# The last two column blocks of a down projection as a seven-product pair, a smaller scratch for GpSimd's DMAs, and what takes its place

## The chip, the cores and the metric

The kernel runs on one core of a Trainium2 chip. The metric is device time in microseconds (us) of one execution; the median of three runs stands for the kernel. The core's engines are TensorE (PE, with its weight loads as PEld), VectorE (DVE), ScalarE (ACT), GpSimd (POOL) and SyncE (SP). Each runs its own instructions in a fixed order and waits on semaphores of the others. In this kernel SP issues the loads of weights, POOL those of a few other things.

## The reference

One layer of a hybrid decoder on 256 tokens of width 2048, all in float32: two gated attention branches, an output projection and a feed-forward block with a causal convolution of width 3.

```python
for l in range(DEPTH):
    h = rms_norm(x, norm_mix_pre[l])
    y = hybrid_mixer(h, w_in[l], ...)            # latent attention + sliding window, gates, w_out
    x = x + rms_norm(y, norm_mix_post[l])
    h = rms_norm(x, norm_ffn_pre[l])
    y = conv_ffn(h, ffn_w_up[l], ..., ffn_w_down[l])
    x = x + rms_norm(y, norm_ffn_post[l])

def conv_ffn(h, w_up, conv_w, conv_b, w_down):
    a, b = jnp.split(h @ w_up, 2, axis=-1)
    ap = jnp.pad(a, ((0, 0), (CONV_WIDTH - 1, 0), (0, 0)))
    c = conv_b
    for j in range(CONV_WIDTH):
        c = c + conv_w[j] * ap[:, j:j + S]
    return (jax.nn.gelu(c, approximate=True) * b) @ w_down
```

The last product, with `w_down` (5632 x 2048), is the down projection. 5632 is 44 rows of 128, 2048 is 4 column blocks of 512.

## The kernel before

**Products.** The 256 tokens are two tiles of 128 (`NT` = 2, index `t`). A float32 operand is split into a high and a low part, and `mm3` adds three matmuls into an accumulator: high by high, high by low, low by high. "A product" below is one `mm3`: 128 rows of weights, one token tile, 512 columns.

**Weights.** They arrive as raw chunks [128 x 1024] of float32, 512 KB each. SP issues the load (L141 or L161), ACT casts the high part (`whi`, L153), DVE subtracts to get the low part (`wlo`, L154), then PE uses both. Raw chunks come from a ring and from lists of further tiles (`more_raw`); converted chunks from a ring of four, with one or two flexible places.

**Pairs of column blocks.** `pair_gemm` (L255) computes two column blocks at once, so that four accumulators (two token tiles by two blocks) are open. Its order string has a letter for each two rows of weights. "p" is a plain unit: two chunks, 8 products, 24 matmuls. "s" is a seven-product unit after Strassen's scheme: 7 products, 21 matmuls. It needs sums of the activations (`g_sums`, `b_sums`, made on DVE) and differences of the weights; it converts three whole chunks and a half. In `seven_parked` the differences were made much earlier and lie in DRAM: `park_sums` (L224) has POOL load two chunks to a staging tile (`load`, L230), four subtractions on DVE (`less`, L234) and POOL store two tiles (L239, L244). At the pair's end four extra accumulators are combined by eight column operations on DVE and ACT (`end_sums`).

**Down projection.** Rows 0 to 23 are done when half of the feed-forward's columns are there, as two pairs ("d0", "d1", with the orders in `PAIR_ORDER`, parked tiles `ta`). Rows 24 to 43 come at the end of the program: blocks 0 and 1 as the pair "db" (`B_ORDER`, six seven-product units, parked tiles `tb`), then block 2 and block 3, each by a plain `gemm` through `down`. After it come, for each token tile, the squares and gains of the second norm (`z_block`), the sum of squares (`z_pre`), the normaliser and the four results with their stores (`finish`). For the second token tile the last block is split, so that its last three rows are done in two halves of 256 columns.

**What sets the order.** `at(tick, f)` puts a piece of work to a tick, and each weight chunk calls `tick()`. Within that the framework's scheduler sets each engine's order from the program's order, priorities and when buffers are free; the result is static. A tile whose buffer is free from the start may so be loaded long before its tick.

**Scratch.** A part of each SBUF partition is set aside for descriptors of DMAs that GpSimd issues; 16 KB by default.

Of the kernel before, what the change touches and what calls it, by code (L numbers as in the profile page):

```python
# [19 lines left out]
P = 128  # L20
# [22 lines left out]
def trunk_layer(ctx, tc, x, x_cols_in, conv_cols_in, g_mix_post, g_ffn_post, w_in, w_q, w_kv,  # L43
# [74 lines left out]
    raw_of = lambda name: ring_tile("raw", name, F32, False)  # L118

# [135 lines left out]
    def pair_gemm(name, w, k0, c0, order, act_of, s_of, kind, d, place=None, sums=None, parked=None):  # L255
# [9 lines left out]

        def plain(u, last):
            for k in (2 * u, 2 * u + 1):
                w_ = convert(raw_row(row(k)), 1024)
                for t in range(NT):
                    for j in range(2):  # L270
                        mul(c[2 * t + j], act_of(k, t), half(w_, j), last and k % 2 == 1)
                tick()

        def seven_parked(u, last):
# [13 lines left out]
            w_ = convert(raw_row(parked[u][1]), 1024)  # L288
            mul(q6, s2, half(w_, 1), last)
            mul(c21, act_of(2 * u + 1, 1), half(w_, 0))  # L290
# [4 lines left out]
        def seven(u, last):  # L295
# [18 lines left out]
            w_ = convert(tb, 1024)  # L314
            mul(q6, s2, half(w_, 0), last)
# [464 lines left out]

    es1.close()
# [29 lines left out]
    tb[1], tb[2] = gate_pair(1)  # L811
    parked_a = [park_a(i, pg, "gr", now[0] + 5 + 5 * i, bufs=2) for i in range(EARLY)]
# [148 lines left out]

    b = now[0] + 2
# [362 lines left out]
    def deep_raws():  # L1325
        turn_flex("w")
        more_raw[:] = [raw_of, f_raw("a"), raw_of, f_raw("b"), raw_of, f_raw("a"), f_raw("b")]

    turn_flex("raw")
    at(now[0] + 8, deep_raws)  # L1330
# [19 lines left out]
    parked_b = [park_sums(f"tb{i}_", w_down, 24 + 2 * i, 0, p6, "gp", now[0] + 6 + 8 * i) for i in range(NB_)]  # L1350
# [11 lines left out]
    def z_block(acc, b, t):  # L1362
# [7 lines left out]
        vec.tensor_tensor(zo, z, gpost2[c0 // 1024][:, c0 % 1024:c0 % 1024 + n], op=ALU.mult)  # L1370
# [12 lines left out]
    def finish(t):  # L1383
# [8 lines left out]
        cuts = range(0, D + 1, 512)  # L1392
        for a, b in zip(cuts[:-1], cuts[1:]):
            vec.scalar_tensor_tensor(dsum_all[t][:, a:b], dsum_all[t][:, a:b], r[:, 0:1], x2_all[t][:, a:b], op0=ALU.mult, op1=ALU.add)
            nc.sync.dma_start(out[t * P:(t + 1) * P, a:b], dsum_all[t][:, a:b])

# [11 lines left out]
    def pair_end(i):  # L1408
        t, j = divmod(i, 2)
        vec.tensor_tensor(dsum[t][j], dsum[t][j], ud[i], op=ALU.add)  # L1410
        z_block(c_db[i], j, t)
# [7 lines left out]
    for i in range(4):  # L1419
        at(now[0] + 2 * i, lambda i=i: pair_end(i))  # L1420
    for i in range(8):
        at(now[0] + 2 * i, lambda i=i: unpark(i // 4, i % 4))
    for j in range(2, 4):
        last = j == 3
        acc, todo = down(24, 20, 512 * j, 512, split=5 if last else None, ps=None if last else (pss, "s"))
        if last:
            z_block(acc[0], 3, 0)
            z_pre(0)
            z_block(acc[0], 4, 0)
            part = [pss.tile([P, 512], F32, name="zb0", tag="s")] + [pst.tile([P, 512], F32, name=f"zb{i}", tag="t") for i in (1, 2)]  # L1430
# [102 lines left out]
```

## Time and profile before

| what | value |
|---|---|
| median of 3 runs | 1461.35 us (1460.38 to 1462.37) |
| the profiled execution | 1461.99 us |
| its span in the profile | 1460.2 us |
| mean granted TensorE clock | 0.999 |
| PE / DVE / ACT / POOL busy | 99 / 77 / 58 / 7% |
| weight chunks of 1024 columns converted on DVE | 501 |
| HBM traffic over the span | 230 GB/s |

The span is the time from the profile's first to its last instruction; the profiled execution's time is longer by what lies around it (1.8 us). In timelines a row has start, duration, engine, source line, operation and tiles, and in brackets the idle time before it and who ended it. A row with "x4" is four instructions run together. Matmuls overlap: the step from one start to the next (the pitch) is what each costs. In the view of windows the columns are length, then busy time of PE, PEld, DVE, ACT and POOL with their instructions, the granted clock, the DMA engines' share and GB/s.

### The profile page before, as it was taken

How to read it: one execution, taken by the hardware profiler on the slowest of the kernel's cores; microseconds unless marked ns; L12 is line 12 of the kernel's file. 1: busy time of each engine (PE TensorE's matmuls, PEld its weight loads, DVE VectorE, ACT ScalarE, POOL GpSimd, SP SyncE). 2: the span in 40 equal slices, each digit the busy share in tenths (PEclk: the TensorE clock that was granted, in tenths of full speed). 3: DMA queues.
4: the chain of work that ended last, by engine and by line, in shares of the span. 5: the costliest groups of instructions: out<-in, count | busy, mean ns of one | idle time of the engine just before them, and what ended most of it. 6: DMA issues, size and time to landing. Idle time of an engine off the chain costs nothing.

```text
span 1460.2 us, 21246 instructions
## 1 busy us (share of the span) xinstructions
PE 1449.6 (99%) x7546; PEld 1238.6 (85%) x7546; DVE 1117.3 (77%) x1953; ACT 850.2 (58%) x1401; POOL 96.4 (7%) x172
## 2 busy tenths in 40 slices
PE   9999999999999999999999999999999999999997
PEld 7888888888888888888888888888888888888886
DVE  7788896766667665768789888876768798876776
ACT  7588874543555554446576565655646565655653
POOL 0012110010000001000000011000000100000000
PEclk9999999999999999999999999999999999999999
DMA  8765376698655559765766789756878888667873
GB/s 303 213 173 164 100 263 195 219 324 257 189 156 160 167 162 333 256 204 163 235 226 213 260 294 315 230 185 221 284 269 299 303 273 296 193 189 252 310 246 130
DMA packets 162438, 336.65 MB, mean 231 GB/s; under 512 B 20075, under 2 KB 31244, under 8 KB 162332
## 3 DMA queue, kind: packets, MB, share of 16 engines
q1 hardware_dynamic: 145600, 276.46, 59.1%
q0 software_dynamic: 16640, 58.78, 11.8%
q8 instruction: 59, 0.97, 0.3%
q14 instruction: 47, 0.39, 0.1%
q10 hardware_dynamic: 92, 0.05, 0.0%
HBM read 308.99 MB, written 26.26 MB: 230 GB/s over the span
## 4 chain that ended last, share of the span: by engine, by line
PE 94%; DVE 3%; ACT 2%; issue 1%; DMA 1%; DVEq 0%; ACTq 0%
PE accg L185 11%; PE accg L187 11%; PE accg L186 11%; PE ub L1263 10%; PE ua L1263 10%; PE ub L1267 5%; PE ua L1267 5%; PE cd L187 2%; PE cd L186 2%; PE cd L185 2%; PE mpo L950 1%; PE cdb L187 1%; PE cdb L185 1%; PE cdb L186 1%; PE cg L185 1%; PE cg L187 1%
## 5 line engine op out<-in xcount | busy, mean ns | idle before, releaser
L154 DVE TENSOR_TENSOR wlo<-raw,whi 128x1024 fp32r<-128x1024 f32 (+2 forms) x485 | 575.3, 1194 | 214.7 <-ACT whi L153 207.3
L153 ACT CAST whi<-raw 128x1024 fp32r<-128x1024 f32 (+2 forms) x485 | 495.0, 1027 | 384.2 <-PE accg L187 155.0
L185 PE MATMUL accg<-whi,ahl 128*128 128x512 f32 (+1 forms) x416 | 162.8, 391 | 0.0
L187 PE MATMUL accg<-whi,ahl 128*128 128x512 f32 (+1 forms) x416 | 160.6, 386 | 0.0
L186 PE MATMUL accg<-wlo,ahl 128*128 128x512 f32 (+1 forms) x416 | 159.8, 384 | 0.0
L1263 PE MATMUL ub<-ahl,whi 128*128 128x512 f32 x640 | 154.7, 391 | 0.1
L1263 PE MATMUL ua<-ahl,whi 128*128 128x512 f32 x640 | 154.6, 391 | 0.0
L185 PE MATMUL accg<-whi,bhl 128*128 128x512 f32 x378 | 148.1, 392 | 0.0
L187 PE MATMUL accg<-whi,bhl 128*128 128x512 f32 x378 | 147.4, 390 | 0.0
L186 PE MATMUL accg<-wlo,bhl 128*128 128x512 f32 x378 | 147.3, 390 | 0.0
L1263 PEld LDWEIGHTS ub<-ahl,whi 128*128 128x128 f32 x640 | 117.5, 188 | 23.0 <-ACT cc L1155 0.4
L1263 PEld LDWEIGHTS ua<-ahl,whi 128*128 128x128 f32 x640 | 117.5, 188 | 22.7
L187 PEld LDWEIGHTS accg<-whi,ahl 128*128 128x128 f32 x416 | 78.1, 188 | 15.4
L186 PEld LDWEIGHTS accg<-wlo,ahl 128*128 128x128 f32 x416 | 78.2, 188 | 13.1
L185 PEld LDWEIGHTS accg<-whi,ahl 128*128 128x128 f32 x416 | 78.2, 188 | 12.9
L1267 PEld LDWEIGHTS ub<-ahl,wlo 128*128 128x128 f32 x640 | 82.3, 191 | 3.2
L1267 PEld LDWEIGHTS ua<-ahl,wlo 128*128 128x128 f32 x640 | 82.2, 191 | 3.1
L1267 PE MATMUL ua<-ahl,wlo 128*128 128x256 f32 x640 | 83.7, 283 | 0.0
L187 PEld LDWEIGHTS accg<-whi,bhl 128*128 128x128 f32 x378 | 71.0, 188 | 14.8
L1267 PE MATMUL ub<-ahl,wlo 128*128 128x256 f32 x640 | 83.3, 283 | 0.0
L186 PEld LDWEIGHTS accg<-wlo,bhl 128*128 128x128 f32 x378 | 71.0, 188 | 14.4
L185 PEld LDWEIGHTS accg<-whi,bhl 128*128 128x128 f32 x378 | 71.0, 188 | 14.4
(575 smaller groups left out, 2417.4 us busy)
## 6 DMA issues: line engine op xcount, KB each, us to landing
raw<-in_ffn_w_up_dram SPq DMA_DIRECT2D x137, 512.0 KB, 4.8
raw<-in_w_in_dram SPq DMA_DIRECT2D x105, 512.0 KB, 4.6
raw<-in_ffn_w_down_dram SPq DMA_DIRECT2D x71, 512.0 KB, 5.0
xraw<-in_ffn_w_up_dram SPq DMA_DIRECT2D x39, 512.0 KB, 5.4
raw<-in_w_o_swa_dram SPq DMA_DIRECT2D x32, 512.0 KB, 5.1
raw<-in_w_o_mla_dram SPq DMA_DIRECT2D x32, 512.0 KB, 5.3
raw<-in_w_out_dram SPq DMA_DIRECT2D x26, 512.0 KB, 4.2
ta_s<-in_ffn_w_down_dram POOLq DMA_DIRECT2D x22, 512.0 KB, 6.1
```

Of the source, the lines that this page charges most:

```text
L153: act.copy(hi[:, a:b], raw[:, a:b])
L154: vec.tensor_tensor(lo[:, a:b], raw[:, a:b], hi[:, a:b].bitcast(F32), op=ALU.subtract)
L185: pe.matmul(o, ah, bh, start=start, stop=False)
L186: pe.matmul(o, ah, bl, start=False, stop=False)
L187: pe.matmul(o, al, bh, start=False, stop=stop)
L950: pe.matmul(o, w(t), p_[:, c], start=n == 0, stop=n == 5)
L1263: pe.matmul(acc[i], hi[:, c], hn[p][:, j * 512:(j + 1) * 512], start=p + j == 0, stop=stop)
L1267: pe.matmul(acc[i][:, 0:256], lo[:, c], hn[p][:, j * 512:j * 512 + 256], start=False, stop=False)
```

## The change

1. *Last two blocks as a pair.* Blocks 2 and 3 of rows 24 to 43 become a third call, "dc", with `B2_ORDER` "ppsspssppp": four seven-product units. Its four parked pairs of differences (`tc`) are made in the attention stage. The activation sums of "db" are used again. The last six chunks are applied to the first token tile only, and kept (`held`); the second tile's products with them are done at the end by `rest`.
2. *One more unit in the first half:* `PAIR_ORDER[0]` goes from "ppppspsspssp" to "pppspsspsssp", with one more parked pair, also in the attention stage. Two of its activation sums are made one column block earlier.
3. *Memory.* The scratch is set to 4096 bytes. In the 12 KB stand a staging tile (`STAGE`, 8 KB in each partition, tag "sg"), used by the later parks in place of a shared one, and a raw chunk (`raw_x`, 4 KB, tag "rx"), added to the lists of raw chunks.
4. *The end.* `z_block` may put its gains later; the column work of "db" is done over four ticks rather than eight, and the residual's reloads (`unpark`) at ticks 8 and 14 of "dc". `finish(0)` leaves two of its four results to be done within the second tile's last `z_block`.

```diff
+    raw_f = lambda name: ring_tile("raw", name, F32, True)
+    raw_x = lambda name: sb(base, [P, 1024], name, tag="rx")
...
-    def convert(raw, n, own=None, parts=None):
+    def convert(raw, n, own=None, parts=None, into=None):
...
-        if own:
+        if into:
+            hi, lo = into
+        elif own:
...
+        chunks, hold = [2 * order.count("p")], len(held) if held else 0
+        left = [order.count("s")]
...
         def plain(u, last):
             for k in (2 * u, 2 * u + 1):
-                w_ = convert(raw_row(row(k)), 1024)
+                chunks[0] -= 1
+                w_ = convert(raw_row(row(k)), 1024, into=into() if hold and chunks[0] == hold - 1 else None)
                 for t in range(NT):
+                    if t and chunks[0] < hold:
+                        held[hold - 1 - chunks[0]] = (act_of(k, 1), w_)
+                        continue
                     for j in range(2):
-                        mul(c[2 * t + j], act_of(k, t), half(w_, j), last and k % 2 == 1)
+                        mul(c[2 * t + j], act_of(k, t), half(w_, j),
+                            chunks[0] == (hold if t else 0) and (j == 1 or not left[0]))
...
+    STAGE = dict(pl=base, tag="sg")
...
+    parked_b2 = []
...
+    for i in range(NB2):
+        parked_b2.append(park_sums(f"tc{i}_", w_down, 24 + 2 * i, 1024, t0=now[0] + 7 + 7 * i, **STAGE))
+    parked_a.append(park_a(EARLY, t0=now[0] + 7 + 7 * NB2, **STAGE))
...
-        more_raw[:] = [raw_of, lambda name: t[:, 0:1024], raw_of, lambda name: t[:, 1024:2048], raw_of]
+        more_raw[:] = [raw_of, lambda name: t[:, 0:1024], raw_of, lambda name: t[:, 1024:2048], raw_of, raw_x]
...
-    for i in range(sum(NA) - EARLY):
-        parked_a.append(park_a(i + EARLY, p6, "gp", now[0] + 8 + 15 * i // 2))
+    for i in range(sum(NA) - EARLY - 1):
+        parked_a.append(park_a(i + EARLY + 1, t0=now[0] + 8 + 15 * i // 2, **STAGE))
...
-            for u in range(2):
-                at(now[0] + 3 + 3 * u, lambda u=u: g_sums(u))
+            for u, t in ((0, 3), (1, 6), (4, 10), (5, 14)):
+                at(now[0] + t, lambda u=u: g_sums(u))
...
-            for u, t in ((4, 0), (5, 4), (2, 8), (3, 11)):
+            for u, t in ((2, 8), (3, 11)):
                 at(now[0] + t, lambda u=u: g_sums(u))
...
     turn_flex("raw")
+    more_raw[:] = [raw_of, raw_x, raw_of, raw_f, raw_of, raw_f]
...
+        def result(j):
+            a, b = 512 * j, 512 * j + 512
+            ins = vec.scalar_tensor_tensor(dsum_all[t][:, a:b], dsum_all[t][:, a:b], r[:, 0:1], x2_all[t][:, a:b], op0=ALU.mult, op1=ALU.add)
+            if j in late:
+                tc.keep_in_program_order(ins)
             nc.sync.dma_start(out[t * P:(t + 1) * P, a:b], dsum_all[t][:, a:b])
...
     for i in range(4):
-        at(now[0] + 2 * i, lambda i=i: pair_end(i))
+        at(now[0] + i, lambda i=i: pair_end(i))
     for i in range(8):
-        at(now[0] + 2 * i, lambda i=i: unpark(i // 4, i % 4))
-    for j in range(2, 4):
...
+        at(now[0] + (8, 14)[i // 4] + i % 4, lambda i=i: unpark(i // 4, i % 4))
+    held = [None] * 6
...
+    c = pair_gemm("dc", w_down, 24, 1024, B2_ORDER, lambda k, t: (GH(k)[:, t * P:(t + 1) * P], GL(k)[:, t * P:(t + 1) * P]),
+                  lambda u: sb_of[u], 1, ud2_tiles, parked=parked_b2, held=held,
+                  into=lambda: [sb(base, [P, 1024], f"wh{k}", F32R, tag=f"ahl{k}") for k in (6, 7)])
+    z_block(c[0], 2, 0)
+    z_block(c[1], 3, 0)
+    z_pre(0)
+    z_block(c[1], 4, 0)
+    for j in range(2):
+        vec.tensor_tensor(dsum[1][2 + j], dsum[1][2 + j], c[2 + j], op=ALU.add)
...
+    rest(part[0], held, 0, 512)
+    z_block(part[0], 2, 1)
+    rest(part[1], held[:-3], 512, 1024)
+    vec.tensor_tensor(dsum[1][3], dsum[1][3], part[1], op=ALU.add)
+    for i in range(2):
+        rest(part[2 + i], held[-3:], 512 + i * 256, 768 + i * 256)
+    rest_of_0 = finish(0, (2, 3))
+    z_block(part[2], 3, 1)
+    z_pre(1)
+    z_block(part[3], 4, 1, rest_of_0)
     finish(1)
...
+B2_ORDER = "ppsspssppp"
+NB2 = B2_ORDER.count("s")
...
-PAIR_ORDER = ("ppppspsspssp", "ppspspsspssp")
+PAIR_ORDER = ("pppspsspsssp", "ppspspsspssp")
...
-    nc = _bacc.Bacc("TRN2", target_bir_lowering=False, num_devices=1)
+    nc = _bacc.Bacc("TRN2", target_bir_lowering=False, num_devices=1, dynamic_dma_scratch_size=4096)
```

The scheduler's order shows what stands where. **At the program's start** SP has the first loads of the input projection; raw_201 is the second row of weights, raw_224 the third, `xr` are columns of the input. Before:

```order
L141 DMA raw_201<-in_w_in_dram 128x2x512
L407 DMA xr_129<-in_x_cols_dram 128x256
L141 DMA raw_224<-in_w_in_dram 128x2x512
L407 DMA xr_130<-in_x_cols_dram 128x256
L141 DMA raw_245<-in_w_in_dram 128x2x512
```

and now:

```order
L143 DMA raw_201<-in_w_in_dram 128x2x512
L421 DMA xr_129<-in_x_cols_dram 128x256
L143 DMA raw_8782<-in_ffn_w_up_dram 128x2x512
L143 DMA raw_224<-in_w_in_dram 128x2x512
L421 DMA xr_130<-in_x_cols_dram 128x256
```

A chunk of the feed-forward's weights (raw_8782, into `raw_x`) has come ahead of raw_224. POOL, in the same place, `gmat` being the norms' gains and `strip` the bias table. Before:

```order
L434 MEMSET ones 128x1
L528 COPY gmat<-gx 128x38
L461 DMA strip<-sel 32x384
L611 DMA bias_646<-strip 128x2x256
L611 DMA bias_734<-strip 128x2x256
```

and now:

```order
L448 MEMSET ones 128x1
L542 COPY gmat<-gx 128x38
L234 DMA tc_s<-in_ffn_w_down_dram 128x1024 x2
L475 DMA strip<-sel 32x384
L625 DMA bias_646<-strip 128x2x256
```

The two loads for the first parked pair of "dc" have become POOL's first DMAs.

**At the program's end** DVE works through the norm. ds_7660 (now ds_7715) holds the first token tile's sums and then results, ds_7661 (now ds_7716) the second's; zb are PE's last accumulators, z the sums that are squared, rz the normaliser. Before:

```order
L1391 SCALAR_TENSOR_TENSOR rz_14281<-wz_14280,yz_14279 128x1
L1394 SCALAR_TENSOR_TENSOR ds_7660<-ds_7660,rz_14281,x2b_13873 128x512 x4
L1433 TENSOR_TENSOR ds_7661<-ds_7661,zb_14234 128x512
L1367 TENSOR_TENSOR z_1_14295<-ds_7661,zb_14235 128x256
L1370 TENSOR_TENSOR ds_7661<-z_1_14295,gpost_1_13368 128x256
L1367 TENSOR_TENSOR z_1_14303<-ds_7661,zb_14236 128x256
L1379 TENSOR_REDUCE zpre_13365<-ssz_13363 128x1
L1370 TENSOR_TENSOR ds_7661<-z_1_14303,gpost_1_13368 128x256
```

and now:

```order
L1418 SCALAR_TENSOR_TENSOR rz_14403<-wz_14402,yz_14401 128x1
L1387 TENSOR_TENSOR z_1_14413<-ds_7716,zb_14348 128x256
L1422 SCALAR_TENSOR_TENSOR ds_7715<-ds_7715,rz_14403,x2b_14121 128x512 x2
L1390 TENSOR_TENSOR ds_7716<-z_1_14413,gpost_1_13437 128x256
L1406 TENSOR_REDUCE zpre_13434<-ssz_13432 128x1
L1387 TENSOR_TENSOR z_1_14421<-ds_7716,zb_14349 128x256
L1407 TENSOR_SCALAR zpre_13434<-zpre_13434 128x1
L1422 SCALAR_TENSOR_TENSOR ds_7715<-ds_7715,rz_14403,x2b_14121 128x512
L1408 TENSOR_SCALAR zpre_13434<-zpre_13434 128x1
L1422 SCALAR_TENSOR_TENSOR ds_7715<-ds_7715,rz_14403,x2b_14121 128x512
L1390 TENSOR_TENSOR ds_7716<-z_1_14421,gpost_1_13437 128x256
```

The first tile's four results stood ahead of the second tile's last sums; now two stand between the last-but-one and the last of these, and two behind the last.

More of the change, by code (lines that the diff above doesn't have):

```diff
@@ L253, in park_a, with pair_gemm @@
         return park_sums(f"ta{i}_", w_down, 2 * u, 1024 * p, pl, tag, t0, **kw)
-    def pair_gemm(name, w, k0, c0, order, act_of, s_of, kind, d, place=None, sums=None, parked=None):
+    def pair_gemm(name, w, k0, c0, order, act_of, s_of, kind, d, place=None, sums=None, parked=None, held=None, into=None):
         c11, c12, c21, c22 = c = banks(kind, f"c{name}_")
@@ L288, in seven_parked @@
             w_ = convert(raw_row(parked[u][1]), 1024)
+            left[0] -= 1
             mul(q6, s2, half(w_, 1), last)
-            mul(c21, act_of(2 * u + 1, 1), half(w_, 0))
+            mul(c21, act_of(2 * u + 1, 1), half(w_, 0), last and 0 < hold == chunks[0])
             tick()
@@ L1348, in b_sums @@
         sb_of[u] = token_sums(gtiles[u].bitcast(F32), a, m, hi, lo)
-    parked_b = [park_sums(f"tb{i}_", w_down, 24 + 2 * i, 0, p6, "gp", now[0] + 6 + 8 * i) for i in range(NB_)]
+    parked_b = [park_sums(f"tb{i}_", w_down, 24 + 2 * i, 0, t0=now[0] + 6 + 8 * i, **STAGE) for i in range(NB_)]
     for c in range(6, 11):
```

60 lines of the change are left out of this document (31 added, 29 removed).

## The prediction

> **What bounds the kernel now.** I read the page first, for which engine fills the span, then what that engine waits for, then single places at the two ends.
>
> ```profile
> span 1460.2 us, 21246 instructions
> ...
> PE 1449.6 (99%) x7546; PEld 1238.6 (85%) x7546; DVE 1117.3 (77%) x1953; ACT 850.2 (58%) x1401; POOL 96.4 (7%) x172
> ...
> PE 94%; DVE 3%; ACT 2%; issue 1%; DMA 1%; DVEq 0%; ACTq 0%
> ```
>
> TensorE is busy 99% of the span and makes 94% of the chain that ended last. The view of waits for PE has three lines in all:
>
> ```profile
> PE warm L78 <- DVE ramp L67: 1.1, 1, 1.1
> PE x2T L1073 <- DVE x L1070: 0.8, 1, 0.8
> PE pstrip L420 <- DMA sel<-in_strip_sel_dram: 0.2, 1, 0.2
> ```
>
> So between the first weights and the last product PE waits 0.8 us in one place, and never for a weight. Two rules follow. A matmul removed anywhere shortens the span by its pitch, provided the weights stay ahead. And a stall added anywhere lengthens it by the whole stall, since PE has no idle time in which to make it up. Outside PE's stretch lie the start (until weights are there) and the tail after PE's last product. The profiled execution took 1461.99 us for a span of 1460.2 us; it lies 0.6 us above the median 1461.35. I put my differences onto the median.
>
> **What is removed.** A seven-product unit makes with 7 products what a plain unit makes with 8, and a product is three matmuls of 512 columns. The order strings hold five more such units (one in pair 0 of the first half, four in the last two blocks): 15 matmuls fewer. The number of 256-column matmuls at the end stays 18. The pitch comes from the chain of waits:
>
> ```profile
> 1340.03 3.65 PE ub L1263 x16
> ```
>
> 3.65/16 = 228 ns, and 15 x 0.228 = **3.4 us** less. It is exact if nothing waits; there is no way to gain more on PE.
>
> **What is added to weight traffic and to DVE.** A seven-product unit converts 3.5 chunks where a plain one converts 2, and each parked pair costs four subtractions. By form (busy us, mean ns):
>
> ```profile
> L154 DVE TENSOR_TENSOR wlo<-raw,whi 128x1024 fp32r<-128x1024 f32 x456 | 555.3, 1223 | 212.1 <-ACT whi L153 205.3 <-PE ua L1263 1.5 <-DMA raw<-in_mla_w_q_up_dram 1.5
> L153 ACT CAST whi<-raw 128x1024 fp32r<-128x1024 f32 x456 | 476.6, 1051 | 375.6 <-PE accg L187 154.3 <-PE cd L187 37.4 <-PE ua L1263 28.3
> ...
> L234 DVE TENSOR_TENSOR ta_s<-ta_s 128x512 f32<-128x512 f32 x44 | 30.2, 685 | 7.0 <-DMA ta_s<-in_ffn_w_down_dram 6.7
> ```
>
> DVE gains 5 x (1.5 x 1.223 + 4 x 0.685) = 22.9 us, ACT 5 x 1.5 x 1.051 = 7.9 us. All of it must lie under PE. The stages it falls into (us; busy of PE, PEld, DVE, ACT, POOL; granted clock, DMA share, GB/s):
>
> ```profile
> 380.00:400.00 20.00, 20.00 (x129) 17.93 (x129) 14.98 (x27) 10.82 (x21) 1.08 (x2) 1.00 0.59 180
> ...
> 1345.00:1397.00 52.00, 52.00 (x233) 43.14 (x233) 41.25 (x51) 33.28 (x42) 0.00 (x0) 1.00 0.91 314
> 1397.00:1452.00 55.00, 55.00 (x253) 45.89 (x251) 37.22 (x52) 24.50 (x37) 0.00 (x0) 1.00 0.53 169
> ```
>
> The 20 subtractions (13.7 us) run in the attention stage, of which the first row is a piece: a quarter of DVE's time is free there. The middle row is the pair of blocks 0 and 1, with six seven-product units among ten, and PE does not stop in it. The new pair has four among ten and pair 0 now six among twelve, both thinner, so what already works at 314 GB/s should work again; the last row, where the new pair goes, has 169 GB/s and a third of DVE unused. The quarter of GpSimd's scratch holds back at most a park whose result is wanted hundreds of us later. The sums of rows 4 and 5 of the first half move one column block earlier, under the same PE. Within the new pair there is one tight place: after its last seven-product unit DVE has eight column operations ahead of a plain chunk's low part, and PE has only the held-over products to go on with. For all this I take 0.2 us; bounds 0 (as the middle row) and 1 (less than two of those 0.685 us operations).
>
> **The start.** The staging tile and the extra raw chunk are free from the first instruction, and the static orders use that. GpSimd's first two DMAs (2 x 512 KB for the new pair) now stand right behind the copy of `gmat`; SP's load of an FFN chunk into the new raw chunk stands ahead of the third row's weights (raw_224). That is 1.57 MB in front of a chunk needed at 12.66 us. First when the queues issue (SP, SP, then GpSimd's copy):
>
> ```profile
> 3.07 0.47 SPq L407 DMA_DIRECT2D xr<-in_x_cols_dram  x1
> 6.27 0.38 SPq L141 DMA_DIRECT2D raw<-in_w_in_dram  x1
> ...
> 3.07 0.21 POOL L528 COPY gmat<-gx 128x38 f32<-128x38 f32 x1 [0.87 <-DMA gx<-in_x_cols_dram]
> ```
>
> The load at 6.27 is raw_224; the new ones need no buffer and go out from 3.3 us on. Then the traffic:
>
> ```profile
> 5.00:10.00 5.00, 5.00 (x18) 3.84 (x18) 3.44 (x6) 3.10 (x6) 0.00 (x0) 1.00 0.78 269
> 10.00:15.00 5.00, 5.00 (x24) 4.14 (x23) 3.58 (x5) 3.72 (x6) 0.00 (x0) 1.00 1.00 340
> 15.00:20.00 5.00, 5.00 (x24) 4.14 (x23) 3.87 (x7) 5.00 (x10) 0.00 (x0) 1.00 1.04 393
> ```
>
> The third row, 393 GB/s, I take as the most the engines carry. In 5 to 10 us (393 - 269) x 5 us = 0.62 MB are spare; the remaining 0.95 MB take 2.4 us, and raw_224 lands so much later. What that chunk's lead is, in one stretch of the timeline:
>
> ```profile
> 10.22 1.05 ACT L153 CAST whi<-raw 128x1024 fp32r<-128x1024 f32 x1 [1.28 <-DMA raw<-in_w_in_dram]
> ...
> 11.30 1.23 DVE L154 TENSOR_TENSOR wlo<-raw,whi 128x1024 fp32r<-128x1024 f32 x1 [1.57 <-ACT whi L153]
> ...
> 12.66 1.07 PE L486 MATMUL acckv<-whi,ahl 128*128 128x512 f32 x4
> 13.56 0.62 PE L486 MATMUL acckv<-wlo,ahl 128*128 128x512 f32 x2
> ```
>
> ACT waits for exactly this DMA; its high part is done at 11.27 (1.39 us before use), the low part at 12.53, 1.03 us before 13.56. So 2.4 - 1.0 = **1.4 us** of stall, bounds 0 (the loads yield, or start late enough to fall behind raw_224) and 3.0 (nothing spare: 1.57 MB / 393 GB/s = 4.0, less 1.0). Nearest rows speak for the middle. Later chunks start from a PE that is itself 1.4 us later, so they are not charged again. Behind the two loads in GpSimd's queue stand only the strip and bias transfers for attention.
>
> [...] The trace of before shows DMA shares of 1.00 and more there, but no load of this size by GpSimd in this stretch.
>
> **The tail.** PE's last product, then DVE's rows for the second token tile:
>
> ```profile
> 1451.99 0.28 PE L187 MATMUL zb<-whi,ghl 128*128 128x256 f32 x1
> ...
> 1448.02 2.74 DVE L1394 SCALAR_TENSOR_TENSOR ds<-ds,rz,x2b 128x512 f32<-128x512 f32 x4
> ...
> 1451.46 0.42 DVE L1367 TENSOR_TENSOR z<-ds,zb 128x256 f32<-128x256 f32 x1
> ...
> 1452.30 0.42 DVE L1367 TENSOR_TENSOR z<-ds,zb 128x256 f32<-128x256 f32 x1
> 1452.64 0.15 DVE L1379 TENSOR_REDUCE zpre<-ssz 128x1 f32<-128x4 f32 x1
> 1452.76 0.42 DVE L1370 TENSOR_TENSOR ds<-z,gpost 128x256 f32<-128x256 f32 x1
> 1453.10 0.14 DVE L1380 TENSOR_SCALAR zpre<-zpre 128x1 f32<-128x1 f32 x1
> ...
> 1453.54 0.21 DVE L1387 TENSOR_SCALAR vz<-ssz,zpre 128x1 f32<-128x1 f32 x1
> ...
> 1454.34 2.74 DVE L1394 SCALAR_TENSOR_TENSOR ds<-ds,rz,x2b 128x512 f32<-128x512 f32 x4
> ```
>
> Call PE's end E = 1452.27. Before, the first tile's four results (2.74 us, 0.68 each) are done under PE's last matmuls; the last sum starts at E + 0.03, its normaliser at E + 1.27, the second tile's results at E + 2.07. In the changed order both column blocks of the first tile end together, and its four results fall among the second tile's last operations: two between the last-but-one and the last sum, two between the last sum and the normaliser. From the second-last part's end (nine half-width matmuls before E, 1.1 us): sum 0.34, two results 1.36, gain 0.34, reduction 0.12: the last sum starts at about E + 1.1 and ends at E + 1.45. Then 0.12 + 0.68 + 0.18 + 0.68 + 0.34 = 2.0 us to the normaliser, at E + 3.45 in place of 1.27: **2.2 us** later. Bounds: 1.4 (only the last two results count) and 2.7 (all four). The results' stores hang on the same rows.
>
> **Sum.** -3.4 + 1.4 + 2.2 + 0.2 = +0.4 us: 1461.35 + 0.4 = **1461.7 us**. With bounds: -3.4 + 0 + 1.4 + 0 = -2.0 to -3.4 + 3.0 + 2.7 + 1 = +3.3, so 1459.4 to 1464.6 for this case alone.
>
> **Rivals.** *A, the start is hidden.* The loads leave raw_224's landing within its lead of 1.0 us. For: the spare 0.62 MB exceeds the FFN chunk, and GpSimd's data may start late. Against: the DMA share is 1.00 from 10 us on. -3.4 + 2.2 + 0.2 gives 1460.4. *B, neither price is paid:* the first tile's sums come out early enough that DVE works its results off before E as well. For: DVE has a third of its time free in the last 55 us. Against: the order is fixed and the sums stand where they stand. -3.4 gives 1458.0. *C, DVE becomes the bound where three seven-product units now follow each other* in pair 0 ("spsspsssp"). Three of them need 10.5 low parts, 12.8 us, in 63 matmuls, 14.4 us. What else DVE does in the stretch 1345 to 1397 is 41.25 - 29 x 1.223 = 5.8 us in 52, or 1.6 us in 14.4: 12.8 + 1.6 already equals 14.4. Once more than the weights' lead falls in there, PE waits: one park's four subtractions, or as many token sums, are 2.7 us. With the forecast's terms +0.4 + 2.7 gives 1464.5, slower. Against: no PE wait for a low part in before, where two such units stand together three times. It decides from the point at which a low part ends after its first use. *D, the stall at the start also costs clock:* PE's only stop in mid-kernel is this one (two rows of the timeline and one of the windows).
>
> ```profile
> 738.98 0.39 PE L186 MATMUL accg<-wlo,bhl 128*128 128x512 f32 x1
> 740.14 0.66 PE L1073 MATMUL x2T<-ident,x 128*128 128x128 f32 x4 [0.77 <-DVE x L1070]
> ...
> 742.00:747.00 5.00, 5.00 (x27) 4.15 (x26) 4.27 (x21) 4.97 (x18) 0.78 (x2) 1.00 1.01 383
> ```
>
> The clock behind 0.77 us of idling is granted in full, so a stall of 1.4 us probably costs itself alone; I leave D at the edge of C, as it would add the difference between half and full pitch for a few matmuls (eight at +0.228: 1.8 us, 1463.5).
>
> **Chances.** Forecast 0.50, A 0.14, B 0.13, C 0.18, D 0.05. About 0.2% (2.9 us) is what a measurement of this kernel tells from no change: faster means under 1458.4, slower above 1464.3. Faster: most of B and a little of A, 0.14. Slower: C but for its low part, the upper edge of the forecast, some of D: 0.22. Same: 0.64. The range that leaves 2 in 10 out cuts most of B and half of C: 1458.7 to 1464.6.
>
> **What would show it.** The start: in the first 20 us a wait of PE for `wlo` or `whi` of the third row, of 1 to 2 us, and GpSimd's loads between 4 and 10 us. The tail: from PE's last matmul to the first of the second tile's four results some 4.2 us instead of 2.07. In between no PE wait over 0.5 us, and stage lengths shorter by 0.7 us in pair 0 and 2.7 us in the last pair. The prediction is wrong if PE shows waits for weights inside a pair, if the third row's weights come in time, or if the tail keeps its length.

## The result and the profile after

The changed kernel took 1464.74 us (median of 12 runs, 1463.07 to 1465.82) against 1461.04 us of the kernel before (12 runs). The ratio is 1.0023 with a 95% interval of 1.0014 to 1.0032: slower by 3.4 us (2.0 to 4.7). The forecast was +0.4 us with bounds up to +3.3; the median lies 0.1 us above the stated range, which ended at 1464.6.

The page of the profile after:

```profile
span 1463.2 us, 21340 instructions
...
PE 1449.8 (99%) x7531; PEld 1236.5 (85%) x7531; DVE 1142.1 (78%) x1992; ACT 861.4 (59%) x1412; POOL 107.2 (7%) x192
...
PE 93%; DVE 2%; DMA 2%; ACT 1%; issue 1%; DVEq 0%; SPq 0%; ACTq 0%
```

PE has 15 matmuls fewer and yet is as long busy (1449.8 against 1449.6 us): it ran some of them more slowly. All waits of PE in that trace:

```profile
PE acckv L500 <- ACT whi L157: 1.7, 1, 1.7
PE warm L78 <- DVE ramp L67: 1.1, 1, 1.1
```

One wait for weights is new, and it is at the start. The windows of the first 25 us show the rest (columns as before the change):

```profile
5.00:10.00 5.00, 5.00 (x16) 3.93 (x15) 3.40 (x6) 2.82 (x6) 0.00 (x0) 1.00 1.03 356
10.00:15.00 5.00, 3.33 (x15) 2.45 (x14) 0.32 (x1) 1.39 (x2) 0.00 (x0) 1.00 1.04 377
15.00:20.00 5.00, 4.93 (x15) 3.55 (x14) 4.83 (x8) 4.52 (x10) 0.00 (x0) 0.66 1.04 395
20.00:25.00 5.00, 5.00 (x24) 4.09 (x23) 4.45 (x9) 5.00 (x9) 0.00 (x0) 1.00 1.05 401
```

Between 10 and 20 us PE started 30 matmuls instead of 48: 18 x 0.228 = 4.1 us. Half of that is the stop ahead of the third row, 2.06 us between two starts; the other half comes after it, where the granted clock is 0.66 and operands come late. The timeline of the changed kernel shows the chain, from the new issues to the third row's products:

```profile
3.57 0.43 SPq L143 DMA_DIRECT2D raw<-in_ffn_w_up_dram  x1
5.99 0.38 SPq L143 DMA_DIRECT2D raw<-in_w_in_dram  x1
...
3.34 1.21 POOL L234 DMA_DIRECT2D tc_s<-in_ffn_w_down_dram  x2
...
13.61 1.05 ACT L157 CAST whi<-raw 128x1024 fp32r<-128x1024 f32 x1 [4.47 <-DMA raw<-in_w_in_dram]
...
12.42 0.61 PE L500 MATMUL accq<-wlo,ahl 128*128 128x512 f32 x2
14.71 1.19 PE L500 MATMUL acckv<-whi,ahl 128*128 128x512 f32 x4 [1.67 <-ACT whi L157]
15.96 0.87 PE L500 MATMUL acckv<-wlo,ahl 128*128 128x512 f32 x2
16.63 1.91 PE L500 MATMUL accq<-whi,ahl 128*128 128x512 f32 x4
...
20.42 0.62 PE L500 MATMUL acckv<-wlo,ahl 128*128 128x512 f32 x2
```

The cast of the third row starts at 13.61 us instead of 10.22, so its chunk landed 3.4 us late. The products begin 2.05 us late (14.71 against 12.66), which is about the 3.4 us less the 1.39 us of lead that the high part had. The four matmuls from 16.63 on take 0.43 us each instead of 0.23.

How the two queues shared the DMA engines meanwhile, the view of DMAs shows for 7 to 11 us (packets, MB, share of the engines' time; q0 is GpSimd's queue, q1 SP's):

```profile
q0 software_dynamic: 253, 0.96, 67.1%
q1 hardware_dynamic: 267, 0.49, 34.2%
```

GpSimd's loads did not fill what SP's left. They took two thirds of the engines' time, with packets about twice as large (3.8 KB against 1.8).

The tail, first PE's last product, then DVE:

```profile
1453.11 0.28 PE L191 MATMUL zb<-whi,ghl 128*128 128x256 f32 x1
...
1452.88 1.41 DVE L1422 SCALAR_TENSOR_TENSOR ds<-ds,rz,x2b 128x512 f32<-128x512 f32 x2
...
1454.61 0.41 DVE L1387 TENSOR_TENSOR z<-ds,zb 128x256 f32<-128x256 f32 x1
...
1457.47 2.74 DVE L1422 SCALAR_TENSOR_TENSOR ds<-ds,rz,x2b 128x512 f32<-128x512 f32 x4
```

E is now 1453.39, the second tile's results start at E + 4.08 (before: 2.07).

Following the same product through both traces gives the ledger of the span's +3.0 us:

| stretch | same product starts, before / after | difference so far | this stretch |
|---|---|---|---|
| start | 16.28 / 20.42 | +4.1 | +4.1 |
| to the FFN-up stage | 806.69 / 809.71 | +3.0 | -1.1 |
| first half's pairs | 1048.45 / 1050.81 | +2.4 | -0.7 |
| pair of blocks 0 and 1 | 1362.69 / 1365.69 | +3.0 | +0.6 |
| last two blocks, to E | 1452.27 / 1453.39 | +1.1 | -1.9 |
| tail | 1454.34 / 1457.47 (results) | +3.1 | +2.0 |

The -1.1 holds the one wait of 0.8 us in the middle of the program; it belongs to the profiled execution of before and not to the change, as the kernel before with a smaller scratch and the same order hasn't it either; the other 0.3 stays open. The +0.6 and the missing 0.8 of the last pair's 2.7 go with weight loads that waited for a low part, as the view of all waits from 1340 us on has it:

```profile
PEld cdc L190 <- DVE wlo L158: 1.1, 3, 0.5
PEld cdb L190 <- DVE wlo L158: 0.8, 2, 0.5
PEld qdb L190 <- DVE wlo L158: 0.4, 2, 0.3
```

The +0.6 belongs to this one execution. In the profiles of five kernels of the next section that have the same pair of blocks 0 and 1 (both loads held back, either one, and both fillings of the gap), the difference to before changes by less than 0.1 us within it. The last two blocks give 1.9 to 2.3 us in them, 1.9 here.

### The profile page after: what moved, and what is told of

Its sections match the earlier page's. It is cut to its first block, busy times and chain, and to the rows that moved or that the text cites. A ratio compares the mean times of both kernels' runs of the same rounds, so it can differ in the third digit from the quotient of the medians.

```text
span 1463.2 us, 21340 instructions
## 1 busy us (share of the span) xinstructions
PE 1449.8 (99%) x7531; PEld 1236.5 (85%) x7531; DVE 1142.1 (78%) x1992; ACT 861.4 (59%) x1412; POOL 107.2 (7%) x192
## 4 chain that ended last, share of the span: by engine, by line
PE 93%; DVE 2%; DMA 2%; ACT 1%; issue 1%; DVEq 0%; SPq 0%; ACTq 0%
PE accg L189 11%; PE accg L191 11%; PE accg L190 11%; PE ua L1282 10%; PE ub L1282 10%; PE ub L1286 5%; PE ua L1286 5%; PE cd L190 2%; PE cd L191 2%; PE cd L189 2%; DMA raw<-in_ffn_w_down_dram 1%; DVE wlo L158 1%; PE mpo L966 1%; PE cg L190 1%; PE cg L189 1%; PE cw L191 1%
## 5 line engine op out<-in xcount | busy, mean ns | idle before, releaser
L158 DVE TENSOR_TENSOR wlo<-raw,whi 128x1024 fp32r<-128x1024 f32 (+2 forms) x499 | 589.0, 1190 | 213.3 <-ACT whi L157 204.5
L157 ACT CAST whi<-raw 128x1024 fp32r<-128x1024 f32 (+2 forms) x499 | 508.3, 1026 | 397.9 <-PE accg L191 153.2
L189 PE MATMUL accg<-whi,bhl 128*128 128x512 f32 x320 | 125.6, 393 | 0.0
L191 PE MATMUL accg<-whi,bhl 128*128 128x512 f32 x320 | 124.8, 390 | 0.0
L190 PE MATMUL accg<-wlo,bhl 128*128 128x512 f32 x320 | 124.7, 390 | 0.0
L191 PEld LDWEIGHTS accg<-whi,bhl 128*128 128x128 f32 x320 | 60.1, 188 | 12.6
L189 PEld LDWEIGHTS accg<-whi,bhl 128*128 128x128 f32 x320 | 60.1, 188 | 12.1
L190 PEld LDWEIGHTS accg<-wlo,bhl 128*128 128x128 f32 x320 | 60.1, 188 | 12.1
```

The costliest lines, as they stand in the source:

```text
L157: act.copy(hi[:, a:b], raw[:, a:b])
L158: vec.tensor_tensor(lo[:, a:b], raw[:, a:b], hi[:, a:b].bitcast(F32), op=ALU.subtract)
L189: pe.matmul(o, ah, bh, start=start, stop=False)
L190: pe.matmul(o, ah, bl, start=False, stop=False)
L191: pe.matmul(o, al, bh, start=False, stop=stop)
```

## The experiments

Each was timed against the kernel before on the same chip; that kernel's medians were 1461.06 to 1461.25 us. Of ten or eleven runs each:

| run | median us | ratio to before, 95% interval |
|---|---|---|
| both loads held back | 1461.05 | 1.0001 (0.9992 to 1.0010) |
| only GpSimd's held back | 1460.41 | 0.9994 (0.9986 to 1.0003) |
| only SP's held back | 1461.99 | 1.0007 (0.9998 to 1.0015) |
| gap filled, 33 matmuls | 1463.52 | 1.0018 (1.0009 to 1.0027) |
| gap filled, 12 matmuls | 1463.85 | 1.0019 (1.0010 to 1.0028) |
| before, with the loads | 1464.58 | 1.0023 (1.0013 to 1.0032) |
| before, 4 KB scratch | 1461.37 | 1.0002 (0.9993 to 1.0011) |
| seven-product units earlier | 1461.37 | 1.0003 (0.9994 to 1.0012) |
| eight chunks kept | 1463.37 | 1.0016 (1.0007 to 1.0024) |
| plain last pair | 1461.95 | 1.0005 (0.9996 to 1.0014) |
| results off DVE | 1463.37 | 1.0015 (1.0006 to 1.0025) |

**Both loads held back.** A tile of the same buffer, with one column written from later data, comes first; all else keeps its order, but for the copies.

```diff
+    sg_hold = sb(base, [P, D], "sg_hold", tag="sg")
+    vec.tensor_copy(sg_hold[:, 0:1], tb[2][0][:, 0:1])
     for i in range(NB2):
...
         t = sb(p3, [P, D], f"xraw{now[0]}", tag="x2_1")
+        if not s_of:
+            rx_hold = raw_x("rx_hold")
+            vec.tensor_copy(rx_hold[:, 0:1], hn[0][:, 0:1].bitcast(F32))
```

> The changed kernel, with one column of the staging tile and of the extra raw chunk written from later data first, so that neither can be loaded at the program's start. Theory (these 1.57 MB in front of the third weight row cost 1.8 us of waiting and 2.3 us of half clock behind it): no PE wait and a granted clock of 1.00 in the first 20 us, PE's products from 20 us on 4.1 us earlier than in the changed kernel, time 1464.7 - 4.1 = 1460.6 us. Rival 1 (the wait at the start has another cause): the wait of 1.7 us stays, 1464.7. Rival 2 (the loads cost as much wherever they stand): the start is clean and 2 us or more come back as waits in the attention stage or the FFN-up stage, 1462.6 or more.

The wait is gone and the granted clock is 1.00 in all windows of the first 25 us; between 10 and 20 us it starts 48 matmuls again:

```profile
10.00:15.00 5.00, 5.00 (x24) 4.12 (x23) 3.23 (x6) 3.95 (x6) 0.00 (x0) 1.00 1.01 347
15.00:20.00 5.00, 5.00 (x24) 4.14 (x23) 4.23 (x8) 4.70 (x10) 0.00 (x0) 1.00 1.04 396
```

The ratio falls by 0.0022, 3.2 us. No wait of 2 us or more came back later: rival 2 falls, rival 1 too.

**Only GpSimd's loads held back, and only SP's.**

> Only GpSimd's two staging loads are held back; SP's 0.5 MB into the extra raw chunk stays ahead of the third weight row. Theory of the sum (spare bandwidth 0.62 MB in 5 to 10 us): nothing is late beyond its lead, 1460.6 us as with both held. Rival (SP's queue works in order, so the whole transfer, 0.52 MB / 393 GB/s = 1.3 us, stands in front, against a lead of 1.0 us): a PE wait of 0.3 us, no half clock, 1460.9.

> Only SP's load into the extra raw chunk is held back; GpSimd's two staging loads (1.05 MB) stay at the start. Theory of the sum: 1.05 - 0.62 = 0.43 MB too much, 1.1 us late against a lead of 1.0 us: a PE wait of 0.1 us, full clock, 1460.7 us. Rival (GpSimd's queue takes more than what is spare while it is active): a PE wait of 1 us or more and a drop of the clock, 1463 us or more.

With SP's load left in place PE does not wait for weights in the first 25 us; the time, 1460.4, is what the sum gives without the start (rival A of the prediction). Yet the load is not free. The cast of the third row starts 1.1 us late (10.22 in the kernel before, 10.61 with both loads held back):

```profile
11.30 1.05 ACT L157 CAST whi<-raw 128x1024 fp32r<-128x1024 f32 x1 [1.45 <-DMA raw<-in_w_in_dram]
```

The sum expected 0, the rival 1.3 us; the chunk's lead just covered it. With GpSimd's loads left in place PE waits 1.1 us, at full clock. That kernel's view of windows, and two rows of its timeline:

```profile
15.00:20.00 5.00, 4.94 (x22) 4.05 (x22) 4.53 (x9) 4.88 (x10) 0.00 (x0) 1.00 1.05 397
```

```profile
12.78 1.04 ACT L157 CAST whi<-raw 128x1024 fp32r<-128x1024 f32 x1 [2.91 <-DMA raw<-in_w_in_dram]
...
13.87 1.19 PE L500 MATMUL acckv<-whi,ahl 128*128 128x512 f32 x4 [1.12 <-ACT whi L157]
```

The cast is 2.6 us late (12.78 against 10.22) where the sum of spare bandwidth said 1.1. From 6 to 11 us the shares of the two queues were:

```profile
q0 software_dynamic: 285, 1.04, 66.5%
q1 hardware_dynamic: 381, 0.60, 35.6%
```

So GpSimd's loads took more than the 0.62 MB that the sum called spare, as the rival had it, while the drop of clock that it expected did not come. Of the two, GpSimd's loads are the costly ones: alone 1.9 us more than SP's alone (ratios 1.0007 and 0.9994, with intervals that still overlap), together with SP's 4.2 us more.

**Filling the gap.**

```diff
+            if k == 2:
+                fill = pst.tile([P, 512], F32, name="fill", tag="t")
+                for _ in range(33):
+                    tc.keep_in_program_order(pe.matmul(fill[:, 0:P], ramp, ramp, start=True, stop=True))
             product(k, acc_kv, w[1])
```

> The changed kernel with 33 matmuls of 128x128 of no use to the result, on constant data, between the second and the third row's products, in PE's gap of 2.06 us. Theory (the half clock from 14.7 to 19.6 us comes from PE's idling): the third row's products still begin at about 14.7 us, the granted clock in 15 to 20 us stays near 1.00 rather than 0.66, time 1464.7 - 2.3 = 1462.4 us. Rival (the half pitch there comes from something else, such as late operands or the DMA load): pitch and time unchanged, 1464.7, or longer by what the fillers add.

The second run has `range(12)` in the same place:

> The changed kernel with 12 matmuls of no use in PE's gap at the start instead of 33: some 0.7 us of the gap of 2.06 us are filled. If the length of the idling decides about the clock (1.50 us between two starts left it full with GpSimd's loads alone at the start, 2.06 us halved it), a rest of 1.4 us leaves it full, and PE's products from 20 us on stand where they stand with 33 fillers, 1463.5 us. If any stop at this place of the program halves it, the pitch of 0.43 us from 16 to 19.6 us stays and the time is 1464.7 us.

With 33 fillers, the fillers' row and the products behind them:

```profile
13.01 2.02 PE L531 MATMUL fill<-ramp 128*128 128x128 bf16 x33
14.89 1.21 PE L500 MATMUL acckv<-whi,ahl 128*128 128x512 f32 x4
...
16.72 1.09 PE L500 MATMUL accq<-whi,ahl 128*128 128x512 f32 x4
```

The third row begins as late as in the changed kernel, and from 16.72 on a matmul takes 0.23 us. With 12 fillers, which leave 1.62 us between two starts, a row of the timeline and one of the windows:

```profile
14.96 1.20 PE L500 MATMUL acckv<-whi,ahl 128*128 128x512 f32 x4 [1.40 <-ACT whi L157]
```

```profile
15.00:20.00 5.00, 4.94 (x20) 3.74 (x21) 4.85 (x7) 4.62 (x10) 0.00 (x0) 1.00 1.06 399
```

Also full clock. The chunk was as late (the third row's products begin at 14.89 and 14.96 us against 14.71) and the DMA engines were as busy from 15 to 20 us as in the changed kernel (shares of 1.07 and 1.06 against 1.04), so of the theory's rivals, late operands and DMA load do not explain the half clock, and of what was tried PE's stop is what is left. After a stop of 1.50 or 1.62 us the clock read 1.00 and after one of 2.06 us 0.66, which agrees with the length deciding; but each is one profiled execution, so the moment at which the stop falls is not excluded.

What the half clock costs was expected as 2.3 us. The products that start at 20.42 us in the changed kernel start here, with 33 and with 12 fillers, at

```profile
19.02 0.61 PE L500 MATMUL acckv<-wlo,ahl 128*128 128x512 f32 x2
...
19.11 0.62 PE L500 MATMUL acckv<-wlo,ahl 128*128 128x512 f32 x2
```

So the traces show 1.4 and 1.3 us. The spans profiled, 1461.0 and 1460.9, are 2.2 and 2.3 us under the changed kernel's, but 0.6 us of that is the pair of blocks 0 and 1, which has nothing to do with the filling. The medians are 1.2 and 0.9 us lower, the ratios 0.0005 and 0.0004 (0.7 and 0.6 us) with intervals that overlap the changed kernel's: the times alone do not show the gain. In how many executions the clock falls stays open. The mean clock that each run lists (0.996 to 0.998 for the changed kernel) does not tell: the profiled execution with 33 fillers lists 0.997, though its granted clock is 1.00 in every stretch of 20 us but the one with PE's end.

**The loads alone, in the kernel before.** First its scratch alone is set to 4096 bytes:

```diff
-    nc = _bacc.Bacc("TRN2", target_bir_lowering=False, num_devices=1)
+    nc = _bacc.Bacc("TRN2", target_bir_lowering=False, num_devices=1, dynamic_dma_scratch_size=4096)
```

> The kernel before with a scratch of 4096 bytes for GpSimd's DMAs, and nothing else changed; every engine's order is the same. Theory (a scratch of a quarter costs nothing, as no DMA of GpSimd's is wanted at once): 1461.2 us, as before, and GpSimd's issues take 0.53 us each. Rival (GpSimd waits for room in it, and parks come later): longer issues, or waits of POOL for its own DMAs, 1462 us or more.

It changes nothing that can be measured (1.0002), and leaves room for the two tiles. Then the loads are put there; nothing reads the tiles, and every other instruction keeps its place:

```diff
+            if k == 2:
+                rx = sb(base, [P, 1024], "rx")
+                nc.sync.dma_start(rx.rearrange("p (a b) -> p a b", a=2), w_up[0:2 * P, 0:512].rearrange("(a p) n -> p a n", p=P))
...
     pool.tensor_copy(gmat, gx[:, 0:38])
+    sg = sb(base, [P, D], "sg")
+    for i in range(2):
+        pool.dma_start(sg[:, i * 1024:(i + 1) * 1024], w_down[(24 + i) * P:(25 + i) * P, 1024:2048])
```

> The kernel before with the scratch of 4096 bytes, and in the room that it leaves nothing but the two suspects: GpSimd's two loads behind the copy of gmat and SP's load of 512 KB ahead of the third weight row, into tiles that nothing reads. All other instructions keep their order on every engine. Theory (these loads alone cost 1.8 us of waiting and 2.3 us of half clock): a PE wait of 1.7 us before the third row's products, a granted clock of about 0.66 in 15 to 20 us, and 1461.2 + 4.1 = 1465.3 us. Rival (the loads hurt only together with something else in the change): no halved clock, 1463 us or less.

PE waits 2.6 us for the third row in the profiled execution; the windows:

```profile
10.00:15.00 5.00, 2.62 (x12) 1.82 (x10) 1.28 (x3) 1.42 (x3) 0.00 (x0) 0.96 1.03 376
15.00:20.00 5.00, 4.75 (x11) 3.79 (x12) 4.64 (x6) 4.60 (x10) 0.00 (x0) 0.50 1.05 399
20.00:25.00 5.00, 5.00 (x20) 4.03 (x20) 4.66 (x9) 5.00 (x10) 0.00 (x0) 0.86 1.05 401
```

The clock is down over all three, and PE is 5.6 us late behind it; this was the slowest of its ten runs (1466.57 us). The median is +3.1 us over the kernel with only the small scratch (ratios 1.0023 and 1.0002), where 4.1 were expected. The loads by themselves make the kernel before about as slow as the changed one.

**The last pair and the tail.** All start from the kernel with GpSimd's loads held back, whose E is 1448.84 and whose second results start at 1452.93, E + 4.09. First another order:

```diff
-B2_ORDER = "ppsspssppp"
+B2_ORDER = "psspsspppp"
```

> As with only the staging loads held back (1460.4 us), and the last pair's order is psspsspppp in place of ppsspssppp: the seven-product units end one plain unit earlier, 5.5 us further from the end. Theory (in the last pair PE loses 0.6 to 0.8 us because DVE's eight column operations after the last seven-product unit stand ahead of low parts, and two of the first tile's results wait behind them): these waits of the weight loads for DVE go, one or two of the results move ahead of the second tile's last sums, and from PE's end to the second tile's results 3.1 to 3.6 us rather than 4.1; time 1459.1 us. Rival (DVE is as late at the pair's beginning, behind the sums of the pair before): the waits only move there, time 1460.0 or more.

The time, 1461.37, is the rival's. In the profiled execution, one of the two slowest of its eleven, the waits grew, now also at the pair's start, where extra accumulators wait for the pair before to be read:

```profile
PE cdc L190 <- DVE wlo L158: 1.1, 2, 0.7
PE qdc L189 <- DVE ds L1389: 1.0, 1, 1.0
```

The tail did shrink, to a little less than the theory's 3.1. PE's last product and the results:

```profile
1452.24 0.28 PE L191 MATMUL zb<-whi,ghl 128*128 128x256 f32 x1
...
1455.49 2.74 DVE L1424 SCALAR_TENSOR_TENSOR ds<-ds,rz,x2b 128x512 f32<-128x512 f32 x4
```

That is E + 2.97. But E, 1452.52, is 3.7 us later than in the kernel that it starts from.

With that order and eight chunks kept:

```diff
-    held = [None] * 6
+    held = [None] * 8
+
+    def held_tiles(i):
+        if i == 0:
+            both = sb(base, [P, D], "wh_sg", F32R, tag="sg")
+            return [both[:, 0:1024], both[:, 1024:2048]]
+        if i == 1:
+            return [sb(p6, [P, 1024], f"wh_f{n}", F32R, tag="f" + n, bufs=2) for n in "ab"]
...
-    rest_of_0 = finish(0, (2, 3))
+    rest_of_0 = finish(0, ())
```

> As the run before with psspsspppp, and the last eight chunks rather than six are kept for the second token tile (two of them converted into the staging tile, two into two buffers of the FFN-up stage, which are free by then), with all four of the first tile's results in their natural place. The first tile's accumulators close 2.7 us earlier before PE's end. Theory (the tail grew by 2.0 us only because the first tile's results are worked off behind the second tile's last sums): none of the first tile's results after PE's end, 2.1 to 2.6 us from PE's end to the second tile's results as in before; time 1459.1 - 1.0 = 1458.1 us, or lower. Rival (DVE has as much work as time in the last 10 us, so that something else is late): 3 us or more from PE's end to the results, and 1459 us or more.

The tail did what the theory says, and the time did not. PE's last product and the results:

```profile
1452.73 0.28 PE L191 MATMUL zb<-whi,ghl 128*128 128x256 f32 x1
...
1455.34 2.74 DVE L1424 SCALAR_TENSOR_TENSOR ds<-ds,rz,x2b 128x512 f32<-128x512 f32 x4
```

That is E + 2.33. But E itself is 4.2 us later, and PE now waits for conversions in the last pair (2.0 us for high parts, 0.8 for a low part), as it has only one token tile's products for each of eight chunks. Then a last pair without seven-product units:

```diff
-B2_ORDER = "ppsspssppp"
+B2_ORDER = "pppppppppp"
...
-    for i in range(4):
-        t, j = divmod(i, 2)
-        at(now[0] + 16 + i // 2, lambda t=t, j=j, i=i: vec.tensor_tensor(dsum[t][2 + j], dsum[t][2 + j], ud2[i], op=ALU.add))
```

> As with only the staging loads held back (1460.4 us), with a last pair of ten plain units, so that its 12 matmuls come back and its four parked pairs and its column operations go. Theory (12 matmuls are worth 12 x 0.228 = 2.7 us, and the seven-product units give back 0.6 us of it in waits): 1460.4 + 2.7 - 0.6 = 1462.5 us; the tail stays at 4.1 us, since it comes from the pair and not from the units. Rival (what the units save in matmuls they lose in conversions and DMAs elsewhere): 1460.4 to 1461 us.

Its last 55 us in the windows, and the row of the second tile's results:

```profile
1395.00:1450.00 55.00, 55.00 (x246) 45.36 (x245) 37.52 (x51) 25.56 (x38) 0.00 (x0) 1.00 0.48 159
```

```profile
1454.80 2.74 DVE L1424 SCALAR_TENSOR_TENSOR ds<-ds,rz,x2b 128x512 f32<-128x512 f32 x4
```

E is 1451.82, 3.0 us later than with the units, and the tail is 2.98, not the 4.1 of the theory. The time, 1461.95, lies between the theory's and the rival's. DVE is busy 37.5 of these 55 us; with the units (same windows of the kernel that this starts from) it is 49.5:

```profile
1395.00:1450.00 55.00, 53.84 (x245) 44.23 (x243) 49.46 (x71) 32.03 (x47) 0.00 (x0) 1.00 0.66 232
```

So about half of the longer tail comes with finishing two blocks together (2.98 against 2.07) and half with DVE's backlog of the units' work (4.09 against 2.98); the kernel with the units moved forward, at 2.97, says the same. The units' net gain is 1.6 us of 2.7 by the ratios (1.0005 and 0.9994), whose intervals overlap. Last, the first tile's results taken off DVE:

```diff
-            ins = vec.scalar_tensor_tensor(dsum_all[t][:, a:b], dsum_all[t][:, a:b], r[:, 0:1], x2_all[t][:, a:b], op0=ALU.mult, op1=ALU.add)
+            if t == 0:
+                ins = act.activation(dsum_all[t][:, a:b], dsum_all[t][:, a:b], AF.Copy, scale=r[:, 0:1])
...
+                pool.tensor_tensor(dsum_all[t][:, a:b], dsum_all[t][:, a:b], x2_all[t][:, a:b], op=ALU.add)
...
-    z_block(part[3], 4, 1, rest_of_0)
+    z_block(part[3], 4, 1)
     finish(1)
+    rest_of_0()
```

> As with only the staging loads held back (1460.4 us), and the first token tile's four results leave DVE: ScalarE multiplies by the normaliser, GpSimd adds the residual, two before and two after the second tile's square root. Theory (the tail is 2.0 us longer because four results, 2.7 us of DVE, stand around the second tile's last sums): 2.1 to 2.7 us from PE's end to the second tile's results, time 1460.4 - 1.6 = 1458.8 us. Rival 1 (ScalarE's multiplications delay the squares and the root by as much): 3.5 us or more from PE's end, 1460 us. Rival 2 (GpSimd's additions, for whose length no row stands in the profiles, end after the second tile's results): the chain ends on GpSimd, 1461 us or more.

DVE's and GpSimd's rows at the end of that kernel:

```profile
1451.01 1.14 DVE L1392 TENSOR_TENSOR ds<-z,gpost 128x256 f32<-128x256 f32 x1
...
1453.57 1.20 DVE L1420 SCALAR_TENSOR_TENSOR rz<-wz,yz 128x1 f32<-128x1 f32 x1
1454.81 3.71 DVE L1430 SCALAR_TENSOR_TENSOR ds<-ds,rz,x2b 128x512 f32<-128x512 f32 x4
...
1450.61 2.67 POOL L1428 TENSOR_TENSOR ds<-ds,x2b 128x512 f32<-128x512 f32 x2 [120.06 <-ACT ds L1425]
...
1453.49 2.49 POOL L1428 TENSOR_TENSOR ds<-ds,x2b 128x512 f32<-128x512 f32 x2 [0.21 <-ACT ds L1425]
```

The time, 1463.37, is above all three expectations. The tail is 4.29, within rival 1's, but for another reason than its. While GpSimd adds, some of DVE's own instructions stretch: 1.14 us where the same took 0.42, 1.20 where it took 0.16, 3.71 for four results where it took 2.74. Of these four only the first is long (1.72 us; the others 0.74 as before), and it alone runs beside an addition. The reduction and the three `TENSOR_SCALAR` at 1452.08 to 1452.92 run beside additions too and take no longer than elsewhere (0.14 to 0.21 us). E is 1.7 us later as well, with more waits of weight loads for low parts in the last pair; why these came stays open.

## Why the prediction failed where it did

**The gain.** Pair 0 became 0.7 us shorter, as forecast for its unit. The last pair gave 1.9 of 2.7 us: waits in it cost some 0.8, within the 0 to 1 allowed, though 0.2 was taken. That they come from the eight column operations behind the last seven-product unit is not shown. The 0.6 in the pair before it did not return in five other profiles.

**The start** is the step that failed: 1.4 us were taken, the profiled execution shows 4.1, and the ratios 3.2. Two terms were wrong. "The remaining 0.95 MB take 2.4 us" assumed that the old traffic has its share first and new loads fill what is spare. It was the other way round: from 7 to 11 us GpSimd's queue had 67% of the engines' time and SP's 34%. The chunk was 3.4 us late for 2.4 by that sum, 2.6 for 1.1 with GpSimd's loads alone, 1.1 for 0 with SP's alone. Each is near what its bytes take at the 393 GB/s of the prediction with nothing spare (4.0, 2.7 and 1.3), which had been the upper bound. Nor were the 393 GB/s reached: in 5 to 10 us the engines carried 356 at a share of 1.03. And the stall was costed as a stall: the half clock behind it was rival D, with a chance of 0.05 and 1.8 us. It was argued from a stop of 0.77 us that left the clock full, which says nothing of one more than twice as long. Its eight matmuls at half pitch were the author's estimate, a number that no row of before shows; the size was about right: 1.3 to 1.4 us by the traces with the gap filled. The first sign named for the start came true, a wait of PE for the third row of 1 to 2 us (1.7); what followed the wait was missing from the sum.

**The second queue.** No row of before could show whether GpSimd's loads take DMA time from SP's, as the kernel before has no load of this size by GpSimd there; that the price would be paid was the author's estimate. The runs show that it is: with GpSimd's loads alone the third row's chunk came 2.6 us late and PE waited 1.1 us, while the two queues' shares of the engines' time, 66.5 and 35.6%, made up the whole.

**The tail** was right: 2.2 us forecast, 2.0 measured, and by the rows named. Its cause was half seen. The order of the results was read rightly, but by two kernels with less of the units' work at the end (2.97 and 2.98) DVE's backlog accounts for half of the lateness.

**The rest.** Rival A's time without the start's price, 1460.4, is what the kernel with GpSimd's loads held back takes. Rival C did not happen: no PE wait in pair 0, where three units follow each other. The scratch is free, as said. No change, within 0.2%, was the likeliest case; the kernel is slower by 0.23% (0.14 to 0.32).

The best version found is the change with GpSimd's first staging loads held back: 1460.41 us, 4.2 us better than the change by the ratios and, at a ratio of 0.9994 (0.9986 to 1.0003), not told apart from the kernel before.

## What to carry to other kernels

A buffer that is free from the first instruction lets a scheduler pull its load to the program's start, where the first weights are still on their way (here GpSimd's two loads, issued from 3.34 us on, and SP's, from 3.57 us on); look there first, and write something late into the tile if it must wait. Bandwidth that looked spare was not kept for the old traffic here: with 0.62 MB called spare the chunk should have come 2.4 us late and came 3.4. Count new loads in full against a chunk's lead, and see what share each queue gets. A stall is priced with what follows it: here the products behind a stop of 2.06 us took 0.43 us a matmul instead of 0.23 for a while, 1.3 to 1.4 us more. Work taken off the matrix engine by more vector work need not be worth its matmuls in full where the vector engine is also the one that ends the program: here the last pair's four units gave a net 1.6 of 2.7 us by the ratios, whose intervals overlap.

## What the runs showed of the hardware

- The clock after a stop of PE, one profiled execution each, the stops beginning 12 to 13.5 us after the start. After 1.50 us between two starts (GpSimd's loads alone) and 1.62 us (12 fillers) the granted clock read 1.00 from 15 to 20 us. After 2.06 us (the changed kernel) it read 0.66 there: by single microseconds 0.70, 0.50, 0.50 and 0.59 from 16 to 20 us, then 1.00, with 0.43 us a matmul. After 3.02 us (the kernel before with the loads: 2.63 us without work, by the windows, behind a matmul of 0.39) it read 0.50 from 15 to 20 us and 0.86 from 20 to 25, with 11 matmuls in 4.75 us of work, 0.43 us each. Whether the same stop lowers the clock in every execution was not tested.
- At the very start, granted clock and pitch do not agree: the clock reads 1.00 from 5 to 10 us in the kernel before, where the six matmuls from 5.57 to 8.30 us take 0.46 us each, against 0.23 from 10 us on. What slows them is not shown.
- GpSimd's 512 KB loads and SP's own chunks did not share the DMA engines evenly: 67% and 34% of their time from 7 to 11 us, with about as many packets each (253 and 267) and twice the bytes in GpSimd's (0.96 and 0.49 MB). SP's chunk came 2.6 us late with GpSimd's two loads alone and 1.1 us late with SP's own extra load of half that size; the second stayed within the chunk's lead and cost no wait.
- Beside GpSimd's additions (2.67 and 2.49 us for two of 128x512 each) some of DVE's instructions took longer in the one profile that has them: a 128x1 `SCALAR_TENSOR_TENSOR` 1.20 us where it took 0.16, a `TENSOR_TENSOR` 1.14 where it took 0.42, and a 128x512 `SCALAR_TENSOR_TENSOR` 1.72 where it took 0.74. A reduction and three `TENSOR_SCALAR` beside the additions kept their length (0.14 to 0.21 us).
